# Rings of four split tiles and a half tile, and 37 more steps of seven products, in a hybrid attention and state-space block

## Chip, cores and metric

The kernel is one launch on one core of a Trainium2 chip. The metric is device time in microseconds (us). TensorE (PE in the profile) multiplies matrices, VectorE (DVE) and ScalarE (ACT) work on elements, GpSimd (POOL) here mainly issues transfers that add to what lies in their target, and SyncE (SP) issues the plain loads.

## What is computed

A residual block over 256 tokens of width 4096, all in float32. One input projection feeds two branches, sparse attention and a Mamba-2 mixer (SSD); each is projected back, weighted by a sigmoid gate, summed, and goes through one output projection.

```python
h = rms_norm(x, pre_norm_gain)
proj = h @ w_in
(q, k, v, gate_a, qi, ki, wi, z, xs, bm, cm, dt_raw, merge_logits) = split(proj)
q, k, qi, ki = (apply_rope(t) for t in (q, k, qi, ki))
y_a = dsa_attention(q, k, v, qi, ki, wi * scale) * silu(gate_a)   # top 64 keys a query
y_b = ssd_mixer(xs, z, bm, cm, dt_raw, ...)                       # conv, scan, gated norm
gates = sigmoid(merge_logits)
merged = gates[0] * (y_a @ w_branch_attn) + gates[1] * (y_b @ w_branch_ssd)
out = x + rms_norm(merged @ w_out, post_norm_gain)
```

## The kernel before

**Products.** TensorE multiplies in `float32r`. To keep float32 accuracy each operand is split into a high part, `h`, a rounded copy made by ScalarE, and a low part, `l`, the difference, made by VectorE. One product is three matmuls of 128x128 by 128x512: low by high, high by low, high by high. The weights are split on the chip as they arrive: a raw tile (`raw`, a ring of `RBUFS` = 8) is loaded, ScalarE copies it into a tile `wh`, VectorE subtracts into `wl`. `wh` and `wl` are rings of `SBUFS` = 5 tiles of [128, 2, 512]; a tile comes free when the last matmul that reads it is done.

**Pairs.** After some plain gemms (`gemm`) at the start come 32 calls of `pair_gemm`, and two plain gemms at the end. A pair makes two blocks of 512 columns for both halves of the tokens, so four outputs, and runs over `plan`, a list of steps. A step covers 256 rows of the weights (four tiles of 128x512, two in each of two raw tiles). It is of one of three kinds:

- S: seven products (21 matmuls) in place of eight, after Strassen and Winograd. The sums of activations that it needs (`ext[i]`, four parts) were made by `make_ext`; the sums of weights are made in the step: one by a transfer of GpSimd that adds to the loaded raw tile (line 586), two by VectorE (lines 607 and 608). Four split tiles are taken: one of the first two weights, one of two more, one with a single weight (half used), one of two.
- D: eight products (24 matmuls), with differences of activations (`ext[i]`, two parts).
- R: eight products from the plain split activations `base[i]`.

A D or R step takes two split tiles. `kinds(seven, pairs, plain)` makes a plan: a step whose number is not in the tuple `seven` is D, one in `seven` is S, or R if it is in `plain`. The tuples are `SX` (attention pairs, z pair 0, gate pair 2, and as `SM` the output pairs), `SS` (SSD pairs, z pair 1, gate pairs 0 and 1), `SY` (branch pairs, eight steps each) and `SG` (gate pairs 3 to 7). The four-part sums lie in big buffers `eb{i}`, one for each number in `SX`; the others in small ones `es{i}`; `set_tags` hands them out.

**Order.** A step's transfers are issued `LEAD` = 2 steps ahead. The pairs run in this order: V/gate (`vg`) 0, QK 1, V/gate 1, QK 2, V/gate 2, QK 3, V/gate 3, z 0, SSD and z pairs (x0, x1, z1, x2, x3), eight gate pairs, eight branch pairs (n, br), three output pairs. What follows a pair (rotation of q and k, attention, convolution and scan, gates) is written as generators in the queue `aux`; `step(pace)` advances it twice in each step of a later pair. An output bank is emptied at the next pair's start (`early`, `late`, `rest`; seven VectorE operations, lines 544 to 570), and the next pair's products take over the banks in the order that `turn` gives. Each engine executes its instructions in the written order.

Of the kernel before, what the change touches and what calls it, by code (L numbers as in the profile page):

```python
# [11 lines left out]
F32 = mybir.dt.float32  # L12
F32R = mybir.dt.float32r
# [4 lines left out]
P = 128  # L18
# [3 lines left out]
NW = 512  # L22
KC = 4
HK = 2
SBUFS = 5
RBUFS = 8
EPS = 1e-6
TOPK = 64
# [2 lines left out]
MASK = -1.0e30  # L31
QSCALE = 128 ** -0.5

SX = (1, 3, 5, 8, 10, 12, 14)
SS = (1, 5, 8, 10, 12, 14)
SY = (1, 4, 6, 9, 12, 14)
SM = SX
SG = (1, 3, 5, 6, 8, 9, 10, 12, 13, 14)
SG_ORDER = (0, 1, 2, 3, 5, 4, 8, 10, 7, 12, 14, 11, 6, 9, 13, 15)
LEAD = 2  # L40
GATES = [((n, br), (n + 1, br)) for n in (0, 2, 4, 6) for br in range(2)]
ISCALE = 32 ** -0.5 * 64 ** -0.5
# [6 lines left out]
def fused_block(tc, x, xT, w_qi, w_misc, w_q0, w_qk, w_vg, w_x, w_z, w_gate, w_br, w_out2, w_out,  # L49
# [7 lines left out]
    yr = root(tc.tile_pool(name="yr", bufs=1))  # L57
    rawp = root(tc.tile_pool(name="rawp", bufs=RBUFS))
    whp = root(tc.tile_pool(name="whp", bufs=SBUFS))
    wlp = root(tc.tile_pool(name="wlp", bufs=SBUFS))  # L60
    pq = root(tc.tile_pool(name="pq", bufs=1, space=bass.MemoryType.PSUM))
# [58 lines left out]
    def drain(upto=None):  # L120
        while aux and (upto is None or upto in aux):
            step()

    def push(gen):
        aux.append(gen)
        return gen
# [28 lines left out]
    def gemm(chunks, nk, act, evac, prep=None, plan=None, done=None, pace=1):  # L155
# [7 lines left out]
        for n, (half, toks) in enumerate(plan):  # L163
# [9 lines left out]
            if half not in parts:  # L173
                wh = whp.tile([P, HK, NW], F32R, tag="wh", name="wh")
                wl = wlp.tile([P, HK, NW], F32R, tag="wl", name="wl")
                parts[half] = wh, wl
                if len(parts) > SBUFS:
                    del parts[next(iter(parts))]
# [59 lines left out]
    def open_pool(name, side="left", bufs=1):  # L238
        cm = tc.tile_pool(name=name, bufs=bufs, side=side)
        return cm, cm.__enter__()  # L240
# [196 lines left out]
    def set_tags(seven):  # L437
        for half in range(2):
            here = range(8 * half, 8 * half + 8)
            big_ = [f"eb{i}" for i in SX if i in here]  # L440
            small = [f"es{i}" for i in here if i not in SX]
            for i in here:
                if i in seven:
                    ext_tag[i] = big_.pop(0)
            for i in here:
                if i not in seven:
                    ext_tag[i] = (small or big_).pop(0)
# [36 lines left out]
        return base[i][:, 0, k, tk], base[i][:, 1, k, tk]  # L484

    def split_tiles(n):
        return (whp.tile([P, n, NW], F32R, tag="wh", name="wh"),
                wlp.tile([P, n, NW], F32R, tag="wl", name="wl"))

# [169 lines left out]
    def kinds(seven, pairs, plain=()):  # L659
        return [(i, "D" if i not in seven else "R" if i in plain else "S") for i in pairs]  # L660
# [11 lines left out]
    def x_of(i, a):  # L672
        V.tensor_add(a, fbit(base[i][:, 0]), fbit(base[i][:, 1]))
        return a
# [6 lines left out]
    def ext_x():  # L681
        for i in range(16):
            make_ext(i, x_of(i, yr.tile([P, 2, S], F32, tag=f"yr{4 + i % 2}", name="fr")), SX)
            yield
# [121 lines left out]
    extb_cm, extb = open_pool("extb", "right")  # L806
    exts_cm, exts = open_pool("exts", "right")
    ext_pool.update(b=extb, s=exts)
    set_tags(SX)
    push(ext_x())  # L810
# [5 lines left out]
    for j in range(4):  # L816
        if j:
            pair_gemm("x", "aux", lambda i: w_qk[j - 1, i], kinds(SX, range(16)), yr4_after(0),
                      ev_qk(j))
# [174 lines left out]
    def x_pair(m, first):  # L994
        pair_gemm("x", "aux", lambda i: w_x[m, i], kinds(SS, range(16)), lambda: yr4(first),
                  ev_x(m), pace=1.25)

    def z_pair(m, seven, outs, hooks={}, pace=1.25):
        pair_gemm("x", "aux", lambda i: w_z[m, i], kinds(seven, range(16)), outs, ev_z(m), hooks,
                  pace)  # L1000

    more = [i for i in SX if i not in SS]
    z_pair(0, SX, yr4_after(0), {more[-1] + 1: lambda: push(remake(
        more, SS, lambda: attp.tile([P, 2, S], F32, tag="lm", bufs=2, name="fr")))}, 1)
    drain()
# [3 lines left out]
    x_pair(1, 4)  # L1009
    z_pair(1, SS, lambda: yr4(4))  # L1010
    x_pair(2, 0)
# [23 lines left out]

    grown = [i for i in SG if i not in SX]

    def grow():
        for n, i in enumerate(grown):
            ext_tag[i] = f"eg{n}"  # L1040
        return remake(grown, SG, lambda: tp.tile([P, 2, S], F32, tag="fr", bufs=2, name="fr"))

    for g, cols in enumerate(GATES):
        last = g == len(GATES) - 1
        if g < 3:
            plan = kinds(SX if g > 1 else SS, range(16))
        else:
            plan = kinds(SG, *((range(16), (6, *range(8, 16))) if last else (SG_ORDER,)))
        if 1 < g and not last:
            plan = [(i, "R" if kind == "D" else kind) for i, kind in plan]  # L1050

        def start_y():
            set_tags(SY)
            push(forms_from("y", load_y, SY, range(16)))

        hooks = {}
        if g == 1:
            hooks[more[-1] + 1] = lambda: push(remake(
                more, SX, lambda: ssdp.tile([P, 2, S], F32, tag="xc", name="fr")))
        if g == 2:  # L1060
            hooks[grown[-1] + 1] = lambda: push(grow())
        if last:
            hooks[4] = start_y
        mode = "DR" if g == 1 else "R" if 1 < g < len(GATES) - 2 else "aux"
        pair_gemm("x", mode, lambda i: w_gate[g, i], plan,
                  lambda: yr4(4 * (g % 2)),
                  ev_gate(cols), hooks, 1.25 if g < 2 else 1)
        if g == 1:
            drain()
            ssdp_cm.__exit__(None, None, None)  # L1070
            tp_cm, tp = open_pool("tp")
            extg_cm, ext_pool["g"] = open_pool("extg")
# [54 lines left out]
    for n in range(0, 8, 2):  # L1127
        for br in range(2):
            pairs = range(8 * br, 8 * br + 8)
            plain = pairs if (n, br) in ((0, 0), (6, 1)) else ()  # L1130
            plan = kinds(SY, pairs, plain)
            hooks = {5: lambda: load_sig(n, br)}
# [14 lines left out]
    ogp = {}  # L1147

    def open_og():
        ogp["cm"], p = open_pool("ogp")  # L1150
        ogp["og"] = [[p.tile([P, 2, NW], F32, name=f"og{t}_{n}") for n in range(3)]
                     for t in range(2)]
        ogp["o6"] = [p.tile([P, NW], F32, name=f"o6_{t}") for t in range(2)]
        ogp["oss"] = p.tile([P, 2, 8], F32, name="oss")
        V.memset(ogp["oss"], 0.0)

# [21 lines left out]

    for n in range(0, 6, 2):
        if n == 0:  # L1180
            order = (0, 2, 4, 6, 7, 1, 9, 3, 8, 5, 11, 10, 12, 13, 14, 15)
            plain = (8, 10, 14)
        else:
            order, plain = range(16), ()
        plan = [(i, "R" if k == "D" else k) for i, k in kinds(SM, order, plain)]

        def done_branch():
            while len(aux) > 1:
                step()
            brp_cm.__exit__(None, None, None)  # L1190
            exts_cm.__exit__(None, None, None)
            open_og()

        pair_gemm("m", "R", lambda i: w_out2[n // 2, i], plan, ogs(n), ev_pair(n),
                  {10: done_branch} if n == 0 else {}, 1 if n else 2)
# [3 lines left out]
    def og(t, n):  # L1199
        if n < 6:  # L1200
            return ogp["og"][t][n // 2][:, n % 2, :]
        return ogp["o6"][t] if n == 6 else yr.tile([P, NW], F32, tag=f"yr{4 + t}", name="o7")

    fin_cm, fin = open_pool("fin")
    res, pgs = {}, {}

    def load_pg(n):
# [43 lines left out]
    def finish_tok(t, ps):  # L1251
        with tc.high_priority():
# [7 lines left out]
         plan=[(h, (0, 1)) for h in range(12)]  # L1260
# [102 lines left out]
```

## Time and profile before

| | |
|---|---|
| median of 3 runs | 2831.57 us (2828.82 to 2831.92) |
| profiled execution | 2833.73 us, span 2832.0 us |
| TensorE busy | 2802.9 us, 12708 matmuls |
| VectorE busy | 2388.5 us, 3122 instructions |
| ScalarE busy | 1739.4 us |
| granted TensorE clock | 0.997 |
| moved by the transfers | 640.72 MB, 226 GB/s on the mean |

A busy time counts overlapping instructions once. TensorE's matmuls are pipelined, so a single one's duration is longer than the distance to the next, and a busy share of 99% alone does not say how densely they follow. The seven or eight products of a step can be followed in the profile at line 539, the splits at lines 492, 494 and 496 and 602 to 610.

### The profile page before, as it was taken

The numbers are of one execution on the slowest core, as the hardware profiler recorded it, in microseconds if no ns is written. First come the engines' busy times: TensorE is split into PE (matmuls) and PEld (weight loads), VectorE is DVE, ScalarE is ACT, GpSimd is POOL, SyncE is SP. The second block draws the span as 40 slices with busy tenths as digits, with TensorE's granted clock in tenths as the row PEclk, the third lists the DMA queues.
The fourth block names the chain that finished last, engine by engine and source line by source line (L and its number), as shares of the span: only waits on it lengthen the run. The fifth ranks groups of instructions, "written<-read, shape, count | busy, mean of one in ns | idle before, by whom it ended". The sixth has DMA issues, their size and how long they took to land.

```text
span 2832.0 us, 36758 instructions
## 1 busy us (share of the span) xinstructions
PE 2802.9 (99%) x12708; PEld 2308.3 (82%) x12708; DVE 2388.5 (84%) x3122; ACT 1739.4 (61%) x2419; POOL 190.0 (7%) x228
## 2 busy tenths in 40 slices
PE   9999999999999999999999999999999999999998
PEld 7877888888888888888888888888887878888886
DVE  6668988888888878988889989999977889878875
ACT  7444565665656656786788656666655555555553
POOL 0100000000000000000000001011000000000000
PEclk9999999999999999999999999999999999999999
DMA  9544776767767676667666788888877787867873
GB/s 373 190 161 164 215 222 202 226 212 223 223 203 224 209 222 213 199 202 214 201 203 189 241 248 243 254 257 252 263 249 239 246 252 241 279 219 231 259 253 134
DMA packets 200428, 640.72 MB, mean 226 GB/s; under 512 B 22576, under 2 KB 23344, under 8 KB 200240
## 3 DMA queue, kind: packets, MB, share of 16 engines
q1 hardware_dynamic: 163728, 567.05, 60.2%
q0 software_dynamic: 28736, 55.59, 11.0%
q10 hardware_dynamic: 7776, 15.73, 1.5%
q8 instruction: 99, 1.62, 0.2%
q14 instruction: 89, 0.73, 0.1%
HBM read 618.36 MB, written 19.92 MB: 225 GB/s over the span
## 4 chain that ended last, share of the span: by engine, by line
PE 89%; DVE 5%; issue 3%; DMA 2%; ACT 1%; SPq 0%; POOL 0%; ACTq 0%; DVEq 0%; POOLq 0%
PE p L539 74%; PE p L195 4%; PE p L196 4%; PE p L197 4%; PE p L365 1%; DVE wl L496 1%; DMA fr<-yscr 1%; DMA mscr<-mT 1%; PE p L903 0%; ACT wh L492 0%; DMA raw<-w_gate_d 0%; DVE wl L187 0%; PE p L770 0%; PE p L737 0%; PE p L396 0%
## 5 line engine op out<-in xcount | busy, mean ns | idle before, releaser
L539 PE MATMUL p<-wh,b 128*128 128x512 f32 x4576 | 1501.3, 393 | 2.6 <-DVE pc L554 2.6
L492 ACT ACTIVATE wh<-raw 128x1024 fp32r<-128x1024 f32 (+1 forms) x1080 | 1040.7, 984 | 660.7 <-PE p L539 322.3
L539 PEld LDWEIGHTS p<-wh,b 128*128 128x128 f32 x4576 | 860.2, 188 | 179.4 <-DVE pc L554 3.0
L496 DVE TENSOR_TENSOR wl<-raw,wh 128x1024 fp32r<-128x1024 f32 (+1 forms) x816 | 892.2, 1101 | 117.6 <-ACT wh L492 101.3
L539 PE MATMUL p<-wl,b 128*128 128x512 f32 x2288 | 892.9, 390 | 1.5 <-DVE wl L494 1.5
L539 PE MATMUL p<-wh,ext 128*128 128x512 f32 x2224 | 747.7, 390 | 0.9 <-ACT wh L492 0.9
L539 PEld LDWEIGHTS p<-wl,b 128*128 128x128 f32 x2288 | 430.6, 188 | 89.6 <-DVE wl L494 3.4
L539 PEld LDWEIGHTS p<-wh,ext 128*128 128x128 f32 x2224 | 418.0, 188 | 88.6 <-ACT wh L492 2.1
L539 PE MATMUL p<-wl,ext 128*128 128x512 f32 x1112 | 435.4, 392 | 1.8 <-DVE wl L496 1.7
L494 DVE SCALAR_TENSOR_TENSOR wl<-raw,wh 128x1024 fp32r<-128x1024 f32 x264 | 322.4, 1221 | 120.1 <-ACT wh L492 117.0
L539 PEld LDWEIGHTS p<-wl,ext 128*128 128x128 f32 x1112 | 209.0, 188 | 50.8 <-DVE wl L496 5.0
L608 DVE TENSOR_TENSOR raw<-raw 128x1024 f32<-128x1024 f32 x184 | 225.2, 1224 | 5.1
L187 DVE TENSOR_TENSOR wl<-raw,wh 128x1024 fp32r<-128x1024 f32 x112 | 138.8, 1240 | 85.2 <-ACT wh L186 84.9
L195 PE MATMUL p<-wh,b 128*128 128x512 f32 x512 | 201.5, 394 | 1.7 <-ACT wh L183 1.7
L196 PE MATMUL p<-wl,b 128*128 128x512 f32 x512 | 199.6, 390 | 0.2 <-DVE wl L184 0.2
L197 PE MATMUL p<-wh,b 128*128 128x512 f32 x512 | 199.3, 389 | 0.0
L186 ACT ACTIVATE wh<-raw 128x1024 fp32r<-128x1024 f32 x112 | 118.3, 1059 | 131.3 <-PE p L197 117.6
L602 ACT ACTIVATE wh<-raw 128x512 fp32r<-128x512 f32 x184 | 114.4, 622 | 76.9 <-PE p L539 76.3
L603 DVE TENSOR_TENSOR wl<-raw,wh 128x512 fp32r<-128x512 f32 x184 | 126.1, 685 | 10.9 <-ACT wh L602 10.9
L607 DVE TENSOR_TENSOR raw<-raw 128x512 f32<-128x512 f32 x184 | 126.8, 689 | 4.6 <-DMA raw<-w_gate_d 0.3
L610 DVE TENSOR_TENSOR wl<-raw,wh 128x512 fp32r<-128x512 f32 x184 | 125.9, 684 | 1.1 <-ACT wh L604 1.1
L195 PEld LDWEIGHTS p<-wh,b 128*128 128x128 f32 x512 | 96.0, 188 | 26.3 <-ACT wh L183 3.6
(243 smaller groups left out, 1812.9 us busy)
## 6 DMA issues: line engine op xcount, KB each, us to landing
raw<-w_gate_d SPq DMA_DIRECT2D x256, 512.0 KB, 5.7
raw<-w_vg_d SPq DMA_DIRECT2D x128, 512.0 KB, 4.9
raw<-w_x_d SPq DMA_DIRECT2D x128, 512.0 KB, 4.9
raw<-w_br_d SPq DMA_DIRECT2D x128, 512.0 KB, 5.0
raw<-w_out_d SPq DMA_DIRECT2D x128, 512.0 KB, 5.2
raw<-w_qk_d SPq DMA_DIRECT2D x96, 512.0 KB, 5.2
raw<-w_z_d SPq DMA_DIRECT2D x64, 512.0 KB, 5.2
raw<-w_qi_d SPq DMA_DIRECT2D x62, 512.0 KB, 5.6
```

Source lines behind the costliest of these rows:

```text
L187: V.tensor_sub(wl, rs, wh.bitcast(F32))
L195: T.matmul(ps[t], al[:, tk], wh[:, i, :], start=first, stop=False)
L196: T.matmul(ps[t], ah[:, tk], wl[:, i, :], start=False, stop=False)
L197: T.matmul(ps[t], ah[:, tk], wh[:, i, :], start=False, stop=last)
L492: A.activation(h, src, AF.Copy, scale=float(sign))
L494: V.scalar_tensor_tensor(l, src, -1.0, fbit(h), ALU.mult, ALU.subtract)
L496: V.tensor_sub(l, src, fbit(h))
L539: T.matmul(ps[j], l, r, start=first and n == 0, stop=left[j] == 0 and n == 2)
L603: V.tensor_sub(l[:, 1, :], ra[:, 1, :], fbit(h[:, 1, :]))
L607: V.tensor_sub(ra[:, 1, :], ra[:, 0, :], ra[:, 1, :])
L608: V.tensor_sub(rb, rb, ra[:, 1:2, :].to_broadcast([P, 2, NW]))
L610: V.tensor_sub(l[:, 0, :], ra[:, 0, :], fbit(h[:, 0, :])))
```

## The change

`SBUFS` becomes 4, and the S step's single-weight split tile comes from a ring of its own, one tile of [128, 1, 512] (`wh1`, `wl1`). The memory goes to two more big buffers: `SX` grows from 7 to 9 numbers, `SS` from 6 to 7, `SY` from 6 to 8 (three of eight to four of eight in a branch pair). `SG` keeps ten numbers, at other places, and the gate pairs 3 to 6 run in the natural order instead of `SG_ORDER`. Of the output pairs the first has six S steps instead of four (with a new order), the others nine instead of seven. The result tile of output block 6 moves into a buffer of the sums. In all, 37 steps become S that were D or R. Line numbers move by up to 3.

```diff
-SBUFS = 5
+SBUFS = 4
...
-SX = (1, 3, 5, 8, 10, 12, 14)
-SS = (1, 5, 8, 10, 12, 14)
-SY = (1, 4, 6, 9, 12, 14)
+SX = (1, 3, 4, 6, 7, 9, 10, 12, 14)
+SS = (1, 3, 6, 9, 10, 12, 14)
+SY = (1, 3, 4, 6, 9, 11, 12, 14)
 SM = SX
-SG = (1, 3, 5, 6, 8, 9, 10, 12, 13, 14)
-SG_ORDER = (0, 1, 2, 3, 5, 4, 8, 10, 7, 12, 14, 11, 6, 9, 13, 15)
+SG = (1, 3, 4, 6, 7, 9, 10, 12, 13, 14)
...
     def split_tiles(n):
+        if n == 1:
+            return (whp.tile([P, 1, NW], F32R, tag="wh1", bufs=1, name="wh"),
+                    wlp.tile([P, 1, NW], F32R, tag="wl1", bufs=1, name="wl"))
...
-            plan = kinds(SG, *((range(16), (6, *range(8, 16))) if last else (SG_ORDER,)))
+            plan = kinds(SG, range(16), (4, 7, *range(8, 16)) if last else ())
...
-        ogp["o6"] = [p.tile([P, NW], F32, name=f"o6_{t}") for t in range(2)]
...
-            order = (0, 2, 4, 6, 7, 1, 9, 3, 8, 5, 11, 10, 12, 13, 14, 15)
-            plain = (8, 10, 14)
+            order = (0, 2, 5, 1, 3, 8, 4, 9, 6, 11, 7, 10, 12, 13, 14, 15)
+            plain = (9, 10, 14)
...
+    o6 = extb.tile([P, 2, NW], F32, tag=f"eb{SX[7]}", name="o6")
```

On VectorE, V/gate pair 1 from step 3. Before, step 3 is S and step 4 is D (`m`, `pc` and `tab` belong to the rotation of q and k that is woven in):

```order
L603 TENSOR_TENSOR wl<-raw,wh 128x512
L693 TENSOR_TENSOR m_4493<-pc,tab 128x4x64
L607 TENSOR_TENSOR raw<-raw 128x512
L695 TENSOR_TENSOR m_4493<-pc,tab 128x4x64
L608 TENSOR_TENSOR raw<-raw 128x1024
L610 TENSOR_TENSOR wl<-raw,wh 128x512
L496 TENSOR_TENSOR wl<-raw,wh 128x512
L496 TENSOR_TENSOR wl<-raw,wh 128x1024
L697 TENSOR_TENSOR pc<-pc,tab 128x512
L494 SCALAR_TENSOR_TENSOR wl<-raw,wh 128x1024
L496 TENSOR_TENSOR wl<-raw,wh 128x1024
```

In the changed kernel, at the same place, from inside step 3 (the splits' lines 492 to 496 and 603 to 610 stand two lines lower):

```order
L610 TENSOR_TENSOR raw<-raw 128x1024
L612 TENSOR_TENSOR wl<-raw,wh 128x512
L498 TENSOR_TENSOR wl<-raw,wh 128x512
L498 TENSOR_TENSOR wl<-raw,wh 128x1024 x2
L605 TENSOR_TENSOR wl<-raw,wh 128x512
L697 TENSOR_TENSOR m_4631<-pc,tab 128x4x64
L609 TENSOR_TENSOR raw<-raw 128x512
L699 TENSOR_TENSOR pc<-pc,tab 128x512
L610 TENSOR_TENSOR raw<-raw 128x1024
L612 TENSOR_TENSOR wl<-raw,wh 128x512
L498 TENSOR_TENSOR wl<-raw,wh 128x512
L700 TENSOR_TENSOR pc<-pc,m_4631 128x512
```

Step 4 is S now and follows an S step: where two splits stood, seven operations stand, between the same rotations.

On VectorE, the start of that pair, where the banks of the QK pair before are emptied. Before:

```order
L494 SCALAR_TENSOR_TENSOR wl<-raw,wh 128x1024
L545 TENSOR_TENSOR pc<-p_3575,pc 128x512
L496 TENSOR_TENSOR wl<-raw,wh 128x1024
L552 TENSOR_TENSOR pc<-p_3502,pc 128x512
L556 SCALAR_TENSOR_TENSOR pc<-p_3502,pc 128x512
L496 TENSOR_TENSOR wl<-raw,wh 128x1024
L603 TENSOR_TENSOR wl<-raw,wh 128x512
L566 SCALAR_TENSOR_TENSOR pc<-p_3509,pc 128x512
```

In the changed kernel:

```order
L496 SCALAR_TENSOR_TENSOR wl<-raw,wh 128x1024
L776 SCALAR_TENSOR_TENSOR yat<-p_4251,sm,pc 128x128 x2
L498 TENSOR_TENSOR wl<-raw,wh 128x1024
L546 TENSOR_TENSOR pc<-p_3597,pc 128x512
L498 TENSOR_TENSOR wl<-raw,wh 128x1024
L547 TENSOR_TENSOR pc<-p_3601,pc 128x512
L605 TENSOR_TENSOR wl<-raw,wh 128x512
L554 TENSOR_TENSOR pc<-p_3528,pc 128x512
L558 SCALAR_TENSOR_TENSOR pc<-p_3528,pc 128x512
L568 SCALAR_TENSOR_TENSOR pc<-p_3535,pc 128x512
```

The operations that empty the banks (`pc<-p`) stand further behind the splits of the new pair, and two operations of the attention before (`yat`) stand among them.

On GpSimd's queue, from the branch pairs to the end. `raw<-w_br_d` and `raw<-w_out_d` are the accumulating transfers of S steps, `fr<-mscr` the loads of merged rows for the output pairs. Before:

```order
L586 DMA raw<-w_br_d 128x512 x6
L1032 DMA fr<-mscr 128x512 x2
L586 DMA raw<-w_br_d 128x512 x12
L1032 DMA fr<-mscr 128x512 x10
L586 DMA raw<-w_out_d 128x512 x18
```

In the changed kernel:

```order
L588 DMA raw<-w_br_d 128x512 x8
L1034 DMA fr<-mscr 128x512 x2
L588 DMA raw<-w_br_d 128x512 x16
L1034 DMA fr<-mscr 128x512 x9
L588 DMA raw<-w_out_d 128x512
L1034 DMA fr<-mscr 128x512
L588 DMA raw<-w_out_d 128x512 x23
```

Each S step has one accumulating transfer; the last load of merged rows moved behind the first of the output pairs.

More of the change, by code (lines that the diff above doesn't have):

```diff
@@ L1201, in og @@
             return ogp["og"][t][n // 2][:, n % 2, :]
-        return ogp["o6"][t] if n == 6 else yr.tile([P, NW], F32, tag=f"yr{4 + t}", name="o7")
+        return o6[:, t, :] if n == 6 else yr.tile([P, NW], F32, tag=f"yr{4 + t}", name="o7")
     fin_cm, fin = open_pool("fin")
+    o6 = extb.tile([P, 2, NW], F32, tag=f"eb{SX[7]}", name="o6")
     res, pgs = {}, {}
```

## Prediction

> **What bounds the kernel now.** I read the page first, then the list of what TensorE waits for, the chain of waits, a table of stages and VectorE's order of time. S is a step of seven products, D or R one of eight; L-numbers are those of the profile.
>
> ```profile
> span 2832.0 us, 36758 instructions
> PE 2802.9 (99%) x12708; PEld 2308.3 (82%) x12708; DVE 2388.5 (84%) x3122; ACT 1739.4 (61%) x2419; POOL 190.0 (7%) x228
> ...
> L539 PE MATMUL p<-wh,b 128*128 128x512 f32 x4576 | 1501.3, 393 | 2.6 <-DVE pc L554 2.6
> ```
>
> ```profile
> PE p L365 <- ACT mT L371: 2.8, 2, 2.0
> PE p L539 <- DVE pc L554: 2.6, 1, 2.6
> ...
> PE p L539 <- DVE wl L496: 1.7, 4, 0.6
> PE p L539 <- DVE wl L494: 1.5, 3, 0.7
> PE p L539 <- ACT wh L492: 0.9, 3, 0.4
> ```
>
> A matmul lasts 393 ns, but 4576 of them cover 1501.3 us, so each spends only part of that alone. TensorE's largest waits are 2.8 us or less in total: it streams nearly from end to end. What one matmul costs is read from a stretch of the chain without a break:
>
> ```profile
> 1950.54 80.82 PE p L539 x354
> ```
>
> 354 matmuls in 80.82 us are 0.228 us each. That, not 0.393, is what a removed matmul returns. [...]
>
> VectorE is the second engine. Its durations overlap too, which its order of time shows in a gate pair (start, duration, line):
>
> ```profile
> 1816.12 0.69 DVE L603 TENSOR_TENSOR wl<-raw,wh 128x512 fp32r<-128x512 f32 x1
> 1816.84 0.69 DVE L607 TENSOR_TENSOR raw<-raw 128x512 f32<-128x512 f32 x1
> 1817.57 1.23 DVE L608 TENSOR_TENSOR raw<-raw 128x1024 f32<-128x1024 f32 x1
> 1818.71 0.68 DVE L610 TENSOR_TENSOR wl<-raw,wh 128x512 fp32r<-128x512 f32 x1
> 1819.31 1.91 DVE L496 TENSOR_TENSOR wl<-raw,wh 128x512 fp32r<-128x512 f32 x2
> 1821.14 1.22 DVE L494 SCALAR_TENSOR_TENSOR wl<-raw,wh 128x1024 fp32r<-128x1024 f32 x1
> 1822.28 2.35 DVE L496 TENSOR_TENSOR wl<-raw,wh 128x1024 fp32r<-128x1024 f32 x2
> 1824.55 0.68 DVE L603 TENSOR_TENSOR wl<-raw,wh 128x512 fp32r<-128x512 f32 x1
> ```
>
> From start to start, 512 elements take 0.60 us and 1024 take 1.14. From L603 to L494 an S step spends 5.02 us, and its first split (half of the 2.27 from 1822.28) 1.13 more: 6.15. A D step is L494 and one L496, 1.14 + 1.13 = 2.27. So **an S step costs VectorE 3.88 us more than a D step** and TensorE three matmuls less, 0.68 us. In time of TensorE an S step is 21 x 0.228 = 4.79 us, a D step 5.48: an S step puts VectorE 1.36 us behind, a D step 3.21 ahead.
>
> Whether VectorE has that time is read by stage. The rows are: the end of the first gemms; the first V/gate pair; QK pair 1; V/gate pairs 1 and 2; one SSD pair; gate pairs 1 and 4; branch pairs (2,0), (2,1), (6,0); output pairs 2 and 4. The first number after the stretch is its length, then TensorE, weight loads, VectorE, ScalarE and GpSimd busy:
>
> ```profile
> 260.00:303.59 43.59, 43.04 (x194) 35.38 (x193) 43.28 (x81) 23.84 (x34) 1.88 (x2) 1.00 0.65 203
> 303.59:387.06 83.47, 83.47 (x372) 68.84 (x371) 72.53 (x84) 49.66 (x61) 6.05 (x7) 1.00 0.73 219
> 387.06:477.28 90.22, 90.22 (x425) 75.15 (x423) 73.97 (x94) 55.42 (x83) 6.06 (x7) 1.00 0.71 212
> 477.28:561.48 84.20, 84.20 (x381) 69.72 (x379) 75.78 (x92) 49.28 (x60) 6.05 (x7) 1.00 0.76 223
> ...
> 651.67:736.13 84.46, 84.46 (x381) 69.56 (x379) 77.50 (x94) 48.24 (x60) 6.08 (x7) 1.00 0.76 227
> 1083.67:1175.32 91.65, 91.65 (x428) 75.89 (x427) 79.38 (x119) 68.84 (x110) 5.18 (x6) 1.00 0.66 200
> 1543.34:1634.12 90.78, 89.21 (x403) 72.67 (x402) 82.86 (x122) 65.24 (x92) 7.14 (x9) 1.00 0.74 230
> 1797.21:1878.04 80.83, 80.80 (x355) 66.27 (x354) 79.33 (x91) 52.07 (x67) 8.67 (x10) 1.00 0.84 250
> 2216.89:2261.39 44.50, 43.64 (x200) 35.84 (x199) 38.91 (x47) 24.39 (x30) 3.74 (x5) 1.00 0.85 267
> 2261.39:2302.87 41.48, 41.48 (x184) 34.36 (x183) 36.42 (x43) 22.30 (x26) 2.62 (x3) 1.00 0.82 255
> 2391.54:2436.44 44.90, 44.03 (x200) 35.77 (x199) 41.16 (x56) 26.99 (x36) 3.92 (x6) 1.00 0.81 253
> 2566.13:2648.41 82.28, 82.28 (x364) 68.13 (x363) 69.50 (x76) 48.21 (x62) 6.04 (x7) 1.00 0.74 228
> 2648.41:2730.86 82.45, 82.45 (x365) 68.30 (x364) 71.39 (x81) 48.12 (x61) 4.32 (x5) 1.00 0.82 263
> ```
>
> The gate pair of 1797.21 already has ten S steps; VectorE is busy 79.33 of 80.83 us there and TensorE loses nothing. So a VectorE share of 98% is no loss by itself, as long as its work lies evenly.
>
> **The change, part by part.** *More S steps.* Seven attention pairs and z pair 0 get 2 each (16), five SSD pairs and gate pairs 0 and 1 get 1 each (7), gate pair 2 gets 2, six of the eight branch pairs 1 each (6), the three output pairs 2 each (6): 37 steps. TensorE: 37 x 3 = 111 matmuls fewer, 111 x 0.228 = **-25.3 us**. VectorE: 37 x 3.88 = +144 us. ScalarE gets three more 512-wide copies a step; its largest busy share above is 75% (68.84 of 91.65), so VectorE stays the one to look at. GpSimd issues 37 more accumulating transfers, SP none more.
>
> *Where VectorE has the time.* Add 3.88 per S step, take 0.68 off the length. QK pair: 73.97 + 7.76 = 81.7 of 88.9. SSD pair: 83.3 of 91.0. Output pairs: 77.3 of 80.9, 79.2 of 81.1. Gate pair 1: 86.7 of 90.1. Branch (2,1): 40.3 of 40.8. All are at or below 99%; the stages themselves lose nothing on the sum.
>
> *Where it has not.* V/gate pair 1: 75.78 + 7.76 = 83.5 of 82.8; pair 2: 85.3 of 83.1. The work is not even either. In this stage lie the previous pair's evacuation and the four rotations of q and k:
>
> ```profile
> L698 DVE TENSOR_TENSOR pc<-pc,m 128x512 f32<-128x512 f32 x4 | 2.7, 685 | 0.0
> L697 DVE TENSOR_TENSOR pc<-pc,tab 128x512 f32<-128x512 f32 x4 | 2.7, 684 | 0.0
> L693 DVE TENSOR_TENSOR m<-pc,tab 128x256 f32<-128x256 f32 x4 | 1.7, 418 | 0.0
> L695 DVE TENSOR_TENSOR m<-pc,tab 128x256 f32<-128x256 f32 x4 | 1.7, 417 | 0.0
> ```
>
> Less the overlap of 0.08 us each, the rotations cost 4 x (0.60 + 0.60 + 0.34 + 0.34) = 7.5 us, and the seven 512-wide operations that empty a pair's banks 7 x 0.60 = 4.2. All of it falls into the first ten steps. There stood 4 S and 6 D: 24.6 + 13.6 + 11.7 = 49.9 us of VectorE against 52.0 of TensorE. Now 6 S and 4 D: 36.9 + 9.1 + 11.7 = 57.7 against 50.7. VectorE falls 7.0 us behind. The pair's 16 x 24 - 7 x 3 = 363 matmuls are 82.8 of its 84.20 us; of the 1.4 us of small matmuls, which give VectorE time, 1.3 lie in these steps: 5.7 remain.
>
> *The ring.* What bridges this is VectorE's lead, and the ring caps it. Between two D steps a tile serves 12 matmuls, 2.74 us; a copy and a subtraction into it take 1.06 and 1.22:
>
> ```profile
> L492 ACT ACTIVATE wh<-raw 128x1024 fp32r<-128x1024 f32 x896 | 924.7, 1056 | 389.7 <-PE p L539 273.8 <-DVE raw L608 84.9 <-issue 15.5
> ```
>
> Five tiles allow 4 x 2.74 - 2.3 = 8.7 us, four 5.9 us. Between S steps the half tile keeps the cap: an S step takes three of four places instead of four of five, and its first tile still waits for the last but one step. So the cut ring costs up to 2.7 us of lead where two D steps meet, at each pair's start. With the full 5.9 the stage loses nothing, with none 5.7. I take a lead of 3 us, because the step before these D steps is an S step, and 3.88 us more work stands in front: 2.7 us lost in each of V/gate pairs 1 to 3, **+8.1** (0 to 17).
>
> *Smaller terms.* The first V/gate pair enters from a stretch where VectorE is busy 43.28 of 43.59 us, so the 2.7 us that the ring took away beforehand are not won back: **+2** (0 to 4). Branch (6,0): 41.16 + 3.88 = 45.0 of 44.2, +1.5; (2,0) and (4,0), 42.8 of 43.8 with an evacuation in front, +0.5 each: **+2.5** (0 to 6). SSD and early gate pairs have small matmuls that wait for chains through VectorE; 0.5 us each in seven, **+3.5** (0, to 7 x 3.9 = 27 if every added step fell on such a chain). Output pairs **+0.5**, for a load of merged rows that now stands behind the first accumulating transfer on GpSimd's queue, and is needed ten steps later. Gate pairs 3 to 6 keep the order of their kinds, ten S of sixteen: 0. Five more sums of activations are of the four-part kind, with a 512-wide subtraction and four of a quarter of it, about 1.4 us in place of 0.7:
>
> ```profile
> L466 DVE TENSOR_TENSOR ext<-fr,ext 128x512 fp32r<-128x512 f32 x22 | 15.1, 685 | 1.2 <-ACT ext L465 1.2
> ```
>
> Two of them fall into the first gemms (in the +2), the others where VectorE has over 3 us to spare: 0. The result tile of block 6 takes the place of sum 12, read last in the pair before: 0. The last two gemms get four tiles; a tile's 2.74 us there stand against 1.22 us of VectorE: 0.
>
> Sum: -25.3 + 8.1 + 2 + 2.5 + 3.5 + 0.5 = **-8.7 us**. The profiled execution took 2833.73 us, 1.7 above its span and 2.2 above the median of the runs; so 2825.0 on its scale and 2822.9 on the median's: **2823**.
>
> **The rivals.** *All of it is hidden.* VectorE stays far enough ahead everywhere. For it: 98% in gate pairs 3 to 6 without loss. Against: the 5.7 us of V/gate. 2831.6 - 25.3 = 2806.
>
> *The lead is gone at the pair's start.* The V/gate pairs lose all 5.7 (17.1 instead of 8.1), the rest as above: -25.3 + 17.1 + 8.5 = +0.3, no change, 2832. For it: the shorter ring; against: in V/gate pair 1 VectorE still waits for ScalarE's copies, and ScalarE for TensorE to free a tile, so a lead is there (the waiting instruction, what it waited for, us in total, times, longest):
>
> ```profile
> DVE wl L494 <- ACT wh L492: 6.3, 5, 1.7
> ```
> ```profile
> ACT wh L492 <- PE p L539: 13.1, 19, 2.1
> ```
>
> *Slower: the accumulating transfer is late.* Each S step needs a third transfer, which starts only when both plain loads have landed:
>
> ```profile
> raw<-w_gate_d SPq DMA_DIRECT2D x256, 512.0 KB, 5.7
> ...
> raw<-w_gate_d POOLq DMA_DIRECT2D x62, 256.0 KB, 5.6
> ```
>
> 5.7 + 5.6 and the issue are some 12 us, against eight raw tiles, which means three steps of VectorE's work: 14.6 us with two S steps among them, but 10.7 with one. Where VectorE is late and then gets its tile late, TensorE pays. The point from which it decides: 25.3 / 37 = 0.68 us lost per added S step. At 1 us each, 2831.6 + 37 - 25.3 = 2843. Against it: ten S steps of sixteen run in the gate pairs without loss. [...]
>
> *Whole durations.* If VectorE could not start an operation before the last had ended, V/gate pair 1 would need 92 operations at their full durations, 75.78 + 92 x 0.08 = 83.1, and two more S steps bring ten operations, 2 x (3.88 + 5 x 0.08) = 8.6: 91.7 of 82.8 us, 8.9 lost in each of three: -25.3 + 26.7 + 8.5 = +10, 2842. [...]
>
> **How the numbers follow.** About 0.2% (5.7 us) is what a measurement of this kernel can tell from no change. Forecast (2814 to 2830): 0.46, of which 0.36 faster and 0.10 same. All hidden (2806 to 2813): 0.20, faster. Lead gone (2829 to 2837): 0.20, of which 0.17 same and 0.03 slower. Late transfers 0.08 and whole durations 0.03, slower; another cause 0.03, of which 0.01 same. Faster 0.56, same 0.28, slower 0.16. The range 2808 to 2836 leaves out the slower cases and the edges of two others.
>
> **What would show it.** The matmuls of the pairs fall from 10200 to 10089. TensorE gets waits for VectorE's `wl` in the V/gate pairs, which then last 84 to 87 us; 82.8 would mean hidden, over 88 the lead gone. QK pairs last 88.9, the gate pair of ten S steps 80.8 as before. Waits of VectorE or ScalarE for raw tiles' transfers in the V/gate pairs would speak for the late transfer. If TensorE's waits rise mostly in the SSD pairs, the 3.5 is the wrong term.

## The result and the profile after

The changed kernel is slower: 2847.68 us (median of 4 runs, 2845.5 to 2850.78) against 2830.76 us of the kernel before on the same chip, a ratio of 1.0056 (95% interval 1.0044 to 1.0069). The profiled execution took 2850.78 us. The forecast was 2823 us, faster, with a range of 2808 to 2836: it came out slower, and above the range.

The head of the page, after:

```profile
span 2849.0 us, 36823 instructions
PE 2795.8 (98%) x12597; PEld 2287.5 (80%) x12597; DVE 2514.9 (88%) x3326; ACT 1801.8 (63%) x2533; POOL 222.1 (8%) x265
```

12708 - 12597 = 111 matmuls are gone, and VectorE has 126.4 us more. But TensorE is busy only 7.1 us less, and the span is 17.0 us longer. The list of what TensorE waits for shows a new first entry: not a split (`wl`) but `pc` at L546 (L544 before), the operation that empties the first output bank of the pair before.

```profile
PE p L541 <- DVE pc L546: 12.8, 5, 3.7
PE p L541 <- DVE wl L496: 8.0, 4, 5.0
PE p L541 <- DVE wl L612: 7.5, 13, 0.9
```

By stage, the rows of V/gate pair 1, QK pair 2, V/gate pairs 2 and 3, SSD pair x0, gate pair 7 and output pairs 0 and 2 (length first, then TensorE, weight loads, VectorE, ScalarE and GpSimd busy, granted clock, transfer share, GB/s):

```profile
477.62:567.98 90.36, 86.06 (x375) 69.00 (x373) 85.09 (x106) 50.96 (x66) 7.07 (x9) 0.98 0.72 215
567.98:656.86 88.88, 88.88 (x419) 73.92 (x417) 77.75 (x99) 58.91 (x89) 8.72 (x11) 1.00 0.78 225
656.86:746.28 89.42, 85.57 (x374) 67.56 (x373) 85.27 (x106) 51.07 (x66) 7.58 (x9) 1.00 0.73 215
835.22:925.77 90.55, 85.80 (x374) 69.00 (x373) 85.34 (x106) 51.18 (x66) 7.80 (x9) 0.98 0.72 215
1014.70:1103.39 88.69, 84.96 (x364) 69.89 (x363) 72.72 (x80) 51.75 (x63) 6.08 (x7) 0.96 0.70 212
2059.06:2149.26 90.20, 87.14 (x376) 69.75 (x374) 71.79 (x109) 50.75 (x69) 7.67 (x13) 1.00 0.73 242
2493.18:2586.11 92.93, 87.92 (x384) 72.21 (x382) 76.75 (x96) 50.79 (x66) 6.10 (x8) 0.96 0.75 226
2586.11:2667.00 80.89, 80.89 (x358) 67.00 (x357) 77.33 (x88) 51.66 (x68) 7.68 (x9) 1.00 0.80 244
```

Of the kernel before, x0, gate pair 7 and output pair 0:

```profile
1000.72:1083.68 82.96, 82.96 (x368) 68.72 (x367) 66.92 (x72) 47.18 (x56) 5.22 (x6) 1.00 0.72 222
2039.71:2126.54 86.83, 85.88 (x376) 70.24 (x375) 70.06 (x102) 49.17 (x68) 7.67 (x13) 1.00 0.77 261
2479.96:2566.13 86.17, 86.17 (x389) 71.48 (x388) 67.72 (x82) 47.20 (x60) 5.19 (x6) 1.00 0.72 228
```

QK pair 2 and output pair 2 show what the change is worth where nothing goes wrong: 88.88 us after 90.19, and 80.9 after 82.28. The loss stands mainly in five stages: V/gate pairs 1 to 3 (84.20, 84.46 and 84.20 before: +17.5 us together), x0 (82.96 before: +5.7) and output pair 0 (86.17 before: +6.8). Those 30.0 us are more than the whole loss of 17.0. Gate pair 7 is 3.4 us longer too, though it has as many matmuls as before; more of it under e2_ring.

What happens at the start of V/gate pair 1 is read from the orders of time of ScalarE, VectorE and TensorE, one fence each (start, duration, line; in brackets the idle time ahead of it and what ended that):

```profile
473.68 0.84 ACTq L790 DMA_DIRECT2D yscr<-yraw  x2
```

```profile
472.43 1.22 DVE L498 TENSOR_TENSOR wl<-raw,wh 128x1024 fp32r<-128x1024 f32 x1
481.69 0.69 DVE L546 TENSOR_TENSOR pc<-p,pc 128x512 f32<-128x512 f32 x1 [8.05 <-DMA yscr<-yraw]
482.30 1.22 DVE L498 TENSOR_TENSOR wl<-raw,wh 128x1024 fp32r<-128x1024 f32 x1
```

```profile
478.75 0.39 PE L541 MATMUL p<-wh,b 128*128 128x512 f32 x1
482.44 0.79 PE L541 MATMUL p<-wh,ext 128*128 128x512 f32 x1 [3.30 <-DVE pc L546]
```

ScalarE issues the two stores of the attention's result (`yscr<-yraw`) at 473.68, just when VectorE comes to its first bank-emptying operation, L546. That stands 8.05 us, until a store has landed. It writes an output tile of the QK pair, and `attend` keeps `yraw` in the same buffers (`yr1`, `yr2`). The splits of the new pair stand behind L546 in VectorE's order and wait with it. TensorE gets no bank for its next product and stands 3.3 us, and VectorE's lead is used up. The kernel before issued the same two stores 5.5 us earlier (9.1 us ahead of the pair's first matmul, where it is 3.9 us here), and its L544 ran at 471.41 without waiting there:

```profile
468.22 0.87 ACTq L788 DMA_DIRECT2D yscr<-yraw  x2
```
```profile
471.41 0.69 DVE L544 TENSOR_TENSOR pc<-p,pc 128x512 f32<-128x512 f32 x1
```

Why the stores are late is in code that the description above tells wrongly. It says that `step(pace)` advances the side work twice in each step. That is true of D and R steps alone; an S step, which does not pass through the loop over `todo`, does it once, in the last line:

```python
                for k, j in todo:
...
                    if (k, j) == todo[3]:
                        step(pace)
            step(pace)
```

The attention enters the queue in step 1 of a QK pair and needs 21 advances: 2 for the scaling, 18 for its parts, and one that issues the stores. `yr4_after`, called in step 15, runs whatever is left at once. Before, steps 1 to 14 held 7 S and 7 D: 7 + 2 x 7 = 21, exactly enough. Now they hold 9 S and 5 D: 9 + 2 x 5 = 19, two short. So the same 37 steps that save matmuls also slow the side work by one advance each. V/gate pairs 1 to 3 and x0 follow the four pairs in which an attention runs at pace 1.

### The profile page after: what moved, and what is told of

It reads as the page before. It is cut to its first block, busy times and chain, and to the rows that moved or that the text cites. A ratio compares the mean times of both kernels' runs of the same rounds, so it can differ in the third digit from the quotient of the medians.

```text
span 2849.0 us, 36823 instructions
## 1 busy us (share of the span) xinstructions
PE 2795.8 (98%) x12597; PEld 2287.5 (80%) x12597; DVE 2514.9 (88%) x3326; ACT 1801.8 (63%) x2533; POOL 222.1 (8%) x265
## 4 chain that ended last, share of the span: by engine, by line
PE 79%; DVE 10%; issue 6%; DMA 3%; ACT 2%; POOL 0%; SPq 0%; DVEq 0%; ACTq 0%; POOLq 0%
PE p L541 66%; PE p L194 3%; PE p L196 3%; PE p L195 3%; DVE wl L498 2%; DVE raw L610 1%; DMA yscr<-yraw 1%; DVE wl L186 1%; DMA fr<-yscr 1%; DVE raw L609 1%; ACT wh L494 1%; DVE wl L612 1%; DMA fr<-mscr 1%; DVE wl L605 1%; PE p L364 0%
## 5 line engine op out<-in xcount | busy, mean ns | idle before, releaser
L541 PE MATMUL p<-wh,b 128*128 128x512 f32 x4330 | 1428.7, 394 | 1.0 <-ACT wh L494 0.5
L498 DVE TENSOR_TENSOR wl<-raw,wh 128x1024 fp32r<-128x1024 f32 (+1 forms) x890 | 953.7, 1088 | 60.4 <-ACT wh L494 53.7
L541 PEld LDWEIGHTS p<-wh,b 128*128 128x128 f32 x4330 | 815.9, 188 | 173.8 <-ACT wh L494 5.0
L541 PE MATMUL p<-wl,b 128*128 128x512 f32 x2165 | 848.0, 392 | 10.3 <-DVE wl L496 8.0
L541 PE MATMUL p<-wh,ext 128*128 128x512 f32 x2396 | 806.9, 392 | 14.1 <-DVE pc L546 12.8
L541 PE MATMUL p<-wl,ext 128*128 128x512 f32 x1198 | 473.8, 395 | 8.3 <-DVE wl L612 7.5
L496 DVE SCALAR_TENSOR_TENSOR wl<-raw,wh 128x1024 fp32r<-128x1024 f32 x227 | 276.9, 1220 | 39.2 <-ACT wh L494 38.1
L610 DVE TENSOR_TENSOR raw<-raw 128x1024 f32<-128x1024 f32 x221 | 270.3, 1223 | 5.6
L604 ACT ACTIVATE wh<-raw 128x512 fp32r<-128x512 f32 x221 | 138.8, 628 | 105.4 <-PE p L541 97.7
L194 PE MATMUL p<-wh,b 128*128 128x512 f32 x512 | 202.1, 396 | 2.0 <-ACT wh L182 2.0
L195 PE MATMUL p<-wl,b 128*128 128x512 f32 x512 | 200.0, 391 | 0.0
L196 PE MATMUL p<-wh,b 128*128 128x512 f32 x512 | 199.8, 390 | 0.0
L605 DVE TENSOR_TENSOR wl<-raw,wh 128x512 fp32r<-128x512 f32 x221 | 151.5, 685 | 16.8 <-ACT wh L604 15.7
L612 DVE TENSOR_TENSOR wl<-raw,wh 128x512 fp32r<-128x512 f32 x221 | 151.1, 684 | 0.0
L606 ACT ACTIVATE wh<-raw 128x512 fp32r<-128x512 f32 x221 | 136.3, 617 | 0.0
```

The lines of the kernel that those rows point to most:

```text
L194: T.matmul(ps[t], al[:, tk], wh[:, i, :], start=first, stop=False)
L195: T.matmul(ps[t], ah[:, tk], wl[:, i, :], start=False, stop=False)
L196: T.matmul(ps[t], ah[:, tk], wh[:, i, :], start=False, stop=last)
L496: V.scalar_tensor_tensor(l, src, -1.0, fbit(h), ALU.mult, ALU.subtract)
L498: V.tensor_sub(l, src, fbit(h))
L541: T.matmul(ps[j], l, r, start=first and n == 0, stop=left[j] == 0 and n == 2)
```

## The experiments

Theory *late chain*: the two missing advances make the store late, its tile holds VectorE, and that costs V/gate pairs 1 to 3 and x0. The rivals were those of the prediction: the shorter ring takes VectorE's lead, or VectorE has too much work there. Output pair 0 needs a cause of its own.

**e1_pace: more advances, all else as changed.**

```diff
-                      ev_qk(j))
+                      ev_qk(j), pace=1.25)
...
-        more, SS, lambda: attp.tile([P, 2, S], F32, tag="lm", bufs=2, name="fr")))}, 1)
+        more, SS, lambda: attp.tile([P, 2, S], F32, tag="lm", bufs=2, name="fr")))}, 1.25)
```

The first place is the call for the QK pairs, the second the one for z pair 0.

> The changed kernel with pace 1.25 instead of 1 in QK pairs 1 to 3 and z pair 0, so that their 19 advances of the side work before the last step become about 23. Theory (late chain): an S step advances the side work once, a D step twice, so nine S steps leave the attention chain two advances short; its tail and its stores to yscr are then written at the pair's end, and VectorE stands some 8 us at the first operation that empties a bank, until the store has let go of the tile. With the faster pace that wait (31.4 us in four places) goes, V/gate pairs 1 to 3 fall from about 90 to 83 to 85 us, x0 from 88.7 to about 83, and the time from 2848 to about 2825. Rival (VectorE's work): the pairs are long because VectorE has more to do than fits; then they stay at 88 us or more and the time falls by less than 5 us.

Measured: 2823.36 us (8 runs) against 2832.05, ratio 0.9970 (0.9960 to 0.9980). VectorE's waits for `yscr<-yraw` are gone from its list, and V/gate pairs 1 and 2, x0 and output pair 0 read:

```profile
476.50:560.09 83.59, 83.59 (x374) 68.04 (x373) 81.65 (x102) 52.00 (x66) 7.78 (x9) 1.00 0.77 230
649.11:732.70 83.59, 83.58 (x374) 68.04 (x373) 81.71 (x102) 52.05 (x66) 7.80 (x9) 1.00 0.80 232
...
994.21:1076.49 82.28, 82.28 (x365) 68.13 (x363) 69.15 (x75) 49.94 (x60) 6.07 (x7) 1.00 0.75 229
2465.45:2557.11 91.66, 87.35 (x384) 71.83 (x383) 76.35 (x95) 50.80 (x66) 6.54 (x8) 0.96 0.77 230
```

Ring and S steps are those of the change; only the number of advances differs. The four places give back 19.6 + 6.4 = 26.0 us of span, and the change turns from slower to faster. The whole remaining price of two more S steps and the shorter ring in a V/gate pair is 0.8 us: 83.59, less the 82.8 that are left of the 84.20 before when two S steps have saved 1.4.

**e10_p106 and e11_p112: the count.** The same two places with a pace of 1.06 (19 x 1.06 = 20.1 advances) and 1.12 (21.3); one run each, beside one of the kernel before (2832.61 us).

> The changed kernel with 1.06 instead of 1 advance of the side work at each step of the three QK pairs and the first projection pair of the SSD. The late chain: the 19 advances between the second and the last step become 20.1, still one short of 21, so the last transfer of the attention output still goes out after the pair's end and its tile is still held when VectorE wants it: V/gate pairs 1 to 3 at 86 to 90 us, wait of VectorE for that transfer 3 to 8 us in each, time 2838 to 2848 us. The rival, that the side work only has to be spread a little more evenly: the gain grows with the pace, a quarter of that at 1.25, so V/gate pairs at 88.5 us and 2842 us.

> The same with 1.12: 21.3 advances, just enough. The late chain: as with 1.25, V/gate pairs 1 to 3 at 83.6 us, no wait of VectorE for the transfer, time 2822 to 2825 us. The rival (gain in proportion to the pace): half of it, V/gate pairs at 87 us, 2835 us.

Measured: 2839.90 and 2823.83 us. The list of what VectorE waits for, with 1.06 and then with 1.12:

```profile
DVE pc L546 <- DMA yscr<-yraw: 24.0, 4, 6.7
```
```profile
DVE pc L546 <- DMA yscr<-yraw: 4.6, 2, 2.5
```

V/gate pair 1 took:

```profile
477.22:567.23 90.01, 86.32 (x374) 69.08 (x373) 85.50 (x107) 50.99 (x66) 7.63 (x9) 0.98 0.71 218
```
```profile
476.94:561.91 84.97, 83.92 (x375) 67.93 (x374) 83.73 (x104) 51.19 (x66) 7.44 (x9) 1.00 0.77 229
```

In proportion to the pace, 1.06 would have given back a quarter in the V/gate pairs. Pair 1 got back 0.35 of its 6.8 us with 1.06, and 5.4 with 1.12. One advance short is nearly as bad as two. The step is not perfectly sharp: x0 fell to 86.07 with 1.06, and with 1.12 two short waits are left.

But it is not the total of 21 that decides. `step` carries fractions over, and what the pace of 0.4 in the V/gate pairs leaves gives the attention of QK pair 2 all 21 advances even with 1.06, the last two of them in the last call of step 14. Its stores still went out only 4.3 us ahead of V/gate pair 2 (at 656.05), as in the pairs with 20 advances, and V/gate pair 2 took 89.97 us:

```profile
651.71 0.81 ACTq L790 DMA_DIRECT2D yscr<-yraw  x2
```

The stores go out 15.0 us ahead of the next pair with 1.25, and 9.1 us ahead with 1.12 and in the kernel before. In these three the last part, which writes `yraw`, has its advance in step 12 or 13; with 1.06 it has it in step 14, in the changed kernel in step 15. The lead of the store is what the advances buy.

**e3_before_late: the fault alone, in the kernel before.** Ring of five, seven S steps, and a pace of 0.9 (21 x 0.9 = 18.9 advances) in the four pairs.

```diff
-                      ev_qk(j))
+                      ev_qk(j), pace=0.9)
...
-        more, SS, lambda: attp.tile([P, 2, S], F32, tag="lm", bufs=2, name="fr")))}, 1)
+        more, SS, lambda: attp.tile([P, 2, S], F32, tag="lm", bufs=2, name="fr")))}, 0.9)
```

> The kernel before, five tiles and seven S steps in the attention pairs, with pace 0.9 instead of 1 in QK pairs 1 to 3 and z pair 0: 21 advances before the last step become about 19, as the nine S steps have. Theory (late chain): the wait for the store appears here too, in four places of 4 to 8 us, V/gate pairs 1 to 3 rise from 84 to 88 to 90 us, x0 from 83 to 87 or more, and the time to 2845 to 2853. Rival (VectorE's work): nothing is added to VectorE, so 2829 to 2833.

Measured: 2844.98 us (5 runs), ratio 1.0048 (1.0036 to 1.0061). V/gate pairs 1 to 3 went to 88.3, 88.9 and 88.6 us, as expected; x0 went to 84.4 only, where I had expected 87 or more. What TensorE and VectorE waited for:

```profile
PE p L539 <- DVE pc L544: 8.3, 4, 3.2
```
```profile
DVE pc L544 <- DMA yscr<-yraw: 25.6, 4, 7.5
```

The kernel before, without an S step more, becomes nearly as slow as the changed one. The late chain alone is sufficient; that it is the store in it is shown by e7_yraw below.

**e2_ring: the ring alone.** The kernel before with `SBUFS = 4` and the half tile.

> The kernel before with only the rings changed (four split tiles and the half tile), all steps as before. Theory (late chain): the rings are not what costs; 2828 to 2835, no stage longer by over 2 us. Rival (the ring): the lead that the fifth tile gave is what is missing, and most of the 17 us shows here, 2840 or more.

Measured: 2836.52 us (11 runs), ratio 1.0018 (1.0009 to 1.0027): about 5 us slower, between the two expectations. V/gate pair 1 and gate pair 7:

```profile
478.92:563.09 84.17, 84.17 (x381) 69.72 (x379) 77.64 (x93) 49.20 (x60) 6.06 (x7) 1.00 0.76 220
```
```profile
2039.11:2131.51 92.40, 88.60 (x377) 71.09 (x376) 72.98 (x107) 50.40 (x69) 8.23 (x14) 0.98 0.74 244
```

Where I had put the ring's price, at the start of V/gate pair 1, it costs nothing (84.17 against 84.20). The largest loss is in gate pair 7 (+5.6 us), where I had expected no stage to grow by over 2. With the shorter ring and the old plan it took 92.4 to 94.6 us in all three kernels (this one and the next two), with the ring of five 86.8 before and 90.7 in e3_before_late. With the shorter ring and the new plan it took from 87.0 (e10_p106) to 91.3 us (e8_y). So it varies by more than 3 us with the same ring, and that the ring lengthens it is not shown. Branch pairs (6,1), +3.9, (0,0), -2.5, and (4,0), -2.8, differ from kernel to kernel with the same ring (the last 44.4 here, 47.6 in e7_yraw). The span of the profiled execution is only 2.2 us longer than before. Where the ring's price of 5 us falls stays open.

**e7a_late and e7_yraw: is it the tile under the store, or the burst of side work?** When the chain is late, its last parts also run all at once. Both kernels are e2_ring with a pace of 0.9; the second also gives `yraw` buffers of its own, so the burst stays and only the sharing goes.

```diff
-        yraw = [yr.tile([P, 2, S], F32, tag=f"yr{1 + i}", name="yraw") for i in range(2)]
+        yraw = [attp.tile([P, 2, S], F32, tag=f"yraw{i}", name="yraw") for i in range(2)]
```

> The kernel before with the ring of four and the half tile, and pace 0.9 in the four pairs: the control for the next one. Late chain: as with five tiles, the wait for the store in four places; the ring's 4.5 us and the late chain's 13 us add to 2847 to 2851.

> The same with pace 0.9, but the attention result that is stored to yscr lies in two tiles of its own instead of yr1 and yr2, which the QK pair's outputs reuse. If it is the store that VectorE waits for, the wait of 25 to 30 us of VectorE goes with the same late chain, the V/gate pairs come back to 84 to 86 us and the time to 2836 to 2841. Rival (the lateness itself): the last operations of the attention stand in VectorE's queue ahead of the banks' emptying whatever tile they write; then TensorE still waits 2 us or more in each place, and the time stays within 3 us of the control.

Measured: 2853.31 us (4 runs, ratio 1.0069, 1.0050 to 1.0087), 2 us above the range expected, and 2838.99 us (10 runs, 1.0022, 1.0013 to 1.0031). V/gate pair 1 with shared and with own buffers:

```profile
477.64:565.22 87.58, 85.72 (x380) 69.08 (x379) 79.55 (x96) 49.12 (x60) 6.06 (x7) 1.00 0.70 217
```
```profile
477.67:561.86 84.19, 84.19 (x381) 69.72 (x379) 77.58 (x94) 49.55 (x60) 6.05 (x7) 1.00 0.76 224
```

V/gate pairs 2 and 3 came to 84.22 and 84.21 us, from 89.99 and 88.95. So in the V/gate pairs the burst is harmless; it is the wait for the store that costs. x0 was not cured (86.87 and 86.79 us). There ScalarE stands for the same store, ahead of a tile of the SSD. `yraw` lies in the attention's pool here, which is closed ahead of x0, so this tile lies in memory that `yraw` leaves:

```profile
ACT rr L888 <- DMA yscr<-yraw: 4.6, 1, 4.6
```

**e5_forms: output pair 0.** In the changed kernel GpSimd issues the last load of merged rows at 2491.28, after waiting for VectorE to finish with the tile; the kernel before had issued its last loads 15 us ahead of the pair. ScalarE then stands 5.36 us for that load, ahead of bank copies and the splits, and TensorE 5.01 us for a split. GpSimd's, ScalarE's and TensorE's order of time, after:

```profile
2491.28 0.55 POOL L1034 DMA_DIRECT2D fr<-mscr  x1 [1.05 <-DVE ext L465]
```
```profile
2497.98 0.63 ACT L471 ACTIVATE b<-fr 128x512 fp32r<-128x512 f32 x1 [5.36 <-DMA fr<-mscr]
2498.51 0.58 ACT L563 ACTIVATE pc<-p 128x512 f32<-128x512 f32 x1
```
```profile
2504.02 0.80 PE L541 MATMUL p<-wl,b 128*128 128x512 f32 x1 [5.01 <-DVE wl L496]
```

Before (GpSimd):

```profile
2464.65 1.18 POOL L1032 DMA_DIRECT2D fr<-mscr  x2 [4.23 <-DVE ext L466]
```

Two more of the forms made ahead of this pair are sums, and all loads go through two `fr` tiles, each held until its form is made. The experiment lets every other load use two buffers of the sums that are free by then.

```diff
     def load_m(i):
-        a = tp.tile([P, 2, S], F32, tag="fr", bufs=2, name="fr")
+        if i % 2:
+            a = exts.tile([P, 2, S], F32, tag=("es0", "es2")[i // 2 % 2], name="fr")
+        else:
+            a = tp.tile([P, 2, S], F32, tag="fr", bufs=2, name="fr")
```

> The changed kernel with every second load of merged rows (load_m) going into a small sum buffer that is free by then (es0 and es2), instead of the two fr tiles alone. Theory: output pair 0 lost 6.8 us because the chain load, split, sums runs through two tiles and has two more sums to make, so the load for form 11 goes out at 2491 us and ScalarE stands 5.4 us at its split, ahead of the copies that empty banks; with four tiles it is early, output pair 0 falls from 92.9 to 85 to 87 us, and the time to about 2841. Rival: the six S steps of that pair are what it cannot feed (VectorE or the accumulating transfers); then it stays over 90 us.

Measured: 2844.43 us (5 runs), ratio 1.0043 (1.0031 to 1.0056). Output pair 0:

```profile
2494.96:2579.82 84.86, 84.86 (x383) 70.28 (x382) 74.59 (x92) 50.05 (x64) 7.07 (x9) 1.00 0.83 245
```

From 92.93 to 84.86 us: 8.1 us. The stage is cured; the span fell by 6.3 us, and the interval of the whole time still overlaps the changed kernel's.

**e6_both: e1_pace and e5_forms together.**

> The changed kernel with both mends, pace 1.25 in the four pairs and the merged rows' loads through four tiles. The late chain and the late forms lie in different stages, so they add: 2823 less the 6.8 us that output pair 0 still loses there gives 2816 to 2818, with output pair 0 at 85 us. If instead the time won in one place only moves the wait on to the next, 2821 or more.

Measured: 2820.09 us (5 runs) against 2832.60, ratio 0.9950 (0.9938 to 0.9963); span 2814.7 against 2832.0. The profiled execution is the fastest of the five, 3.6 us below their median: by the medians 12.5 us are won, by the spans 17.3. The time lies between my two expectations, above the 2816 to 2818; output pair 0 came to 84.85 us, as expected. TensorE is busy 18.5 us less than before:

```profile
PE 2784.4 (99%) x12597; PEld 2282.3 (81%) x12597; DVE 2515.0 (89%) x3326; ACT 1804.5 (64%) x2533; POOL 222.1 (8%) x265
```

**e8_y: e6_both, and the same remedy for the loads of `y` ahead of the first branch pairs** (odd loads below 8 into a tile `fg` in `load_y`).

> As the kernel with both mends, and the loads of the first eight rows of branch activations (load_y) alternate between the fr tiles and one tile of the pool that the gate pairs leave unused in gate pair 7. Gate pair 7 and branch pair (0,0) take 136.2 us with the faster pace against 135.7 before, though TensorE has no matmul more or less there; ScalarE stands 31 us for these loads. If the chain of two tiles is the reason, the two stages fall by 2 to 4 us and the time by as much against the kernel with both mends; if the ring of four tiles is (the kernel with only the ring changed has 92.4 in gate pair 7 against 86.8), under 1 us.

Measured: 2816.82 us (5 runs), ratio 0.9939 (0.9927 to 0.9952). Its interval overlaps that of e6_both, and the spans are 2814.4 and 2814.7. Gate pair 7 and branch pair (0,0), in e6_both and then in e8_y:

```profile
2033.40:2121.07 87.67, 86.23 (x376) 70.12 (x375) 72.31 (x109) 51.39 (x70) 7.66 (x13) 1.00 0.75 248
2121.07:2168.62 47.55, 45.03 (x193) 35.73 (x192) 33.58 (x44) 25.34 (x31) 3.38 (x5) 1.00 0.77 246
```
```profile
2032.53:2123.82 91.29, 88.10 (x376) 72.05 (x375) 77.41 (x119) 54.22 (x75) 8.21 (x14) 0.96 0.78 255
2123.82:2168.40 44.58, 43.83 (x193) 35.97 (x192) 28.32 (x34) 21.87 (x26) 3.15 (x4) 1.00 0.79 248
```

135.22 and 135.87 us together, not 2 to 4 us less: no gain is shown, and the two tiles are not shown to be the reason. How much of the loss stands in which of the two stages differs. Both kernels beat the kernel before and the changed one.

## Why the prediction was wrong, step by step

- **The matmuls (-25.3 us): right.** The pairs' matmuls fell from 10200 to 10089. QK pair 2 lost 1.31 us and output pair 2 1.4, for two S steps at 0.68 each; branch pair (2,1) lost 0.68 for one (41.48 to 40.80). The stream pays 0.228 us a matmul.
- **V/gate pairs 1 to 3 (+8.1 us): the step that failed.** The stages came out at 89.4 to 90.6 us, and by the prediction's own reading "over 88" meant that the lead was gone, by VectorE's added work and the cut ring. The lead was gone, but for another reason. What I priced, work and ring, costs 0.8 us a pair (e1_pace), 2.4 in three, inside the 0 to 17 but far below 8.1. Part of the reason is that I sized VectorE's work too high: two S steps took it from 75.78 to 81.65 us in V/gate pair 1 of e1_pace, 5.9 us and not 7.76, which fits into the stage, and the whole change gave it 126.4 us and not 144. My 3.88 took the distances inside one S step, two of which are 0.72 us for 512 elements; four operations at 0.60 and three at 1.14, less the 2.27 of a D step, are 3.55, and 126.4 / 37 is 3.4. What I did not price is that a step is also a place where side work is advanced. I counted the matmuls, splits and transfers of an S step, and took for granted that it advances the side work twice like any other. The lost advances cost 19.6 us in the three pairs.
- **x0 (no term of its own): missed for the same reason.** It sat in the 0.5 us for an SSD pair. It took 5.7 us more, and 6.4 of its 88.69 us went with e1_pace.
- **A hint was in the order shown.** The order of the changed kernel had two `yat` operations, the attention's last on VectorE, among the splits just ahead of the first bank-emptying operation. I read them as a shift in VectorE's order. They say that the attention is not done when the pair's last step begins: its transposition and its stores are still to come. The waits of the kernel before held a warning too: there VectorE already stood 1.3 us for this very store, once:

```profile
DVE pc L545 <- DMA yscr<-yraw: 1.3, 1, 1.3
```

- **Output pairs (+0.5 us): right place, wrong size, and half the mechanism.** The load that "now stands behind the first accumulating transfer" was the one that came late. But it did not wait for GpSimd's queue: its releaser is VectorE's work on the tile's last content. Measured: 8.1 us (92.93 against 84.86).
- **The ring (2.7 us in each V/gate pair): wrong place.** Alone it costs about 5 us, and none of it in V/gate pair 1; where it falls is not shown.
- **First V/gate pair (+2): right.** 84.32 us in e6_both, after 83.47 before; with the 1.37 of its two S steps that is 2.2.
- **SSD and early gate pairs (+3.5): about right.** x0, x1, z1, x2, x3, g0 and g1 together are 1.0 us longer in e6_both than before, in spite of 7 x 0.68 = 4.8: 5.8 us.
- **Branch pairs (+2.5): not seen.** Without the two faults the eight took 346.0 us instead of 353.4, that is 3.3 better than 6 x 0.68. Pair (6,0), for which I wanted 1.5, went from 44.90 to 44.20. Pairs (0,0), (4,0) and (6,1) vary by 3 us or more between kernels that change nothing there, so of these 3.3 us I can put none down to the S steps.
- **The rivals.** No wait of VectorE, and only 2.7 us of ScalarE's, is for raw tiles of the gate pairs, and none for those of the attention pairs: the late accumulating transfer did not come. (By the code it needs only the first of the two plain loads to have landed; I wrote both.) Whole durations did not come either: VectorE is busy 81.65 of 83.59 us in e1_pace with the V/gate pair 0.8 us from its floor. The slower case that did come had no entry but the 0.03 for "another cause".

Put together: the changed kernel without the two faults (e6_both) is 12.5 us below the kernel before by the medians and 17.3 by the profiled spans, where the prediction's terms summed to -8.7. The two faults cost 26 and 8 us, and -17.3 + 34 is the 17 by which the span of the changed kernel grew.

## What to carry to other kernels

When steps are exchanged for steps of another kind, count what each kind does for others: how often it advances side work, and how much slack that count had; here it had exactly none. For every buffer that is reused under an outgoing transfer, find the last point at which the transfer may be issued, because the first write into it can hold an engine, as L546 held VectorE for 8.05 us here, and with it the splits that stand behind in the engine's order. And where one order of instructions shows operations of an old chain among those of the next stage, follow that chain to its end before pricing anything else.

## What the runs showed of the hardware

A stand of 3.3 us cost TensorE more than 3.3 us. The stretches of the changed kernel after the stand at V/gate pair 1, with the granted clock as the third number from the end:

```profile
478.98:482.44 3.46, 0.16 (x1) 0.00 (x0) 0.74 (x2) 0.00 (x0) 0.00 (x0) 0.99 0.97 268
482.44:485.60 3.16, 3.16 (x8) 2.48 (x9) 3.16 (x5) 0.00 (x0) 0.00 (x0) 0.50 0.01 2
485.60:488.67 3.07, 3.07 (x14) 2.55 (x13) 3.07 (x7) 0.33 (x1) 0.00 (x0) 0.97 0.00 0
```

For 3.16 us the clock was 0.50, and 8 matmuls ran in the time of 14: 3.16 - 8 x 0.228 = 1.3 us more. Not every stand in these runs was followed by the low clock, and the length did not tell which was. At V/gate pair 2, where TensorE stood 2.2 us for the same operation, the stage's clock stayed at 1.00 (its row is in the table of stages above). In e3_before_late TensorE stood 2.20 us for that operation at V/gate pair 1 and 3.18 us at V/gate pair 2. The 3.80 us behind each:

```profile
481.01:484.81 3.80, 3.80 (x10) 3.01 (x11) 3.80 (x7) 0.00 (x0) 0.00 (x0) 0.55 0.00 0
660.50:664.30 3.80, 3.80 (x16) 2.85 (x17) 3.80 (x7) 0.00 (x0) 0.00 (x0) 1.00 0.00 0
```

The shorter stand was followed by the low clock, 10 matmuls in the time of 16, and the longer one was not. What decides it is not shown.

The rows of the changed kernel show one thing more: while VectorE stood, the transfers ran on at 268 GB/s, and afterwards they moved next to nothing for 6 us. That the raw tiles were then all full is the likely reason; it was not tried apart.

The two stores' time from issue to landing went with how late they were issued. The list of transfers gives a median of 3.3 us before and of 8.1 in the changed kernel:

```profile
yscr<-yraw ACTq DMA_DIRECT2D x8, 256.0 KB, 3.3
```
```profile
yscr<-yraw ACTq DMA_DIRECT2D x8, 256.0 KB, 8.1
```

It is 3.5 to 5.5 us in the other kernels that issue them about 9 us or more ahead of the next pair (e6_both, e8_y, e1_pace, e2_ring, e11_p112), and 6.7 to 7.9 in the others that issue them 3 to 5 us ahead (e3_before_late, e7_yraw, e7a_late, e10_p106, e5_forms). Why a late store also takes longer was not tried.
